# Eight seam norms of a recurrent diffusion backbone, computed with tokens on partitions instead of channels

## The chip, the core and the metric

The kernel runs on one core of a Trainium2 chip. The metric is device time in microseconds (us) of one execution; the profile is that of one profiled execution of the same program, its stretches given in us from the start of its span. Engines are named as in the profile: PE (matmuls), PEld (their weight loads), DVE, ACT, POOL, and the DMA queues SPq and POOLq.

## What is computed

Two groups of tokens, 128 of a context and 512 of a latent grid, pass through two layers of 1024 channels. Each layer is twice the same frame: a norm, a large block (three recurrent mixers, or a gated feed-forward net), and a gated residual. After both layers comes a last norm.

```python
def rmsnorm(x, w):
    y = x * lax.rsqrt(jnp.mean(x * x, axis=-1, keepdims=True) + EPS)
    return y * w

def trunk_layer(x, cvec, lp, init, rows):
    sh1, sc1, g1, sh2, sc2, g2 = jnp.split(silu(cvec) @ lp["w_ada"] + lp["b_ada"], 6)
    h = rmsnorm(x, lp["norm1"]) * (1 + sc1) + sh1
    mix, states = mixer(h, lp, init, rows)
    x = x + g1 * mix
    h = rmsnorm(x, lp["norm2"]) * (1 + sc2) + sh2
    a, b = jnp.split(h @ lp["w_gu"], 2)
    return x + g2 * ((silu(a) * b) @ lp["w_down"]), states
# after two layers: rmsnorm(x, norm_f)
```

The mean is over the 1024 channels of a token. The mixer also uses `a = -exp(s_a_log)`.

## The kernel before

Channels lie on partitions, tokens on columns: `x[k]` (k = 0 to 7) is a 128 x 640 tile of 128 channels by all 640 tokens, and every matmul takes 320 columns, half of the tokens (`HALF`; half 0 holds the context and the first 192 latent tokens, half 1 the rest). Large products are made in three matmuls each, with weights split in a high and a low part (`wh`, `wl`, made by one ACT and one DVE instruction of 128 x 1024) and inputs split likewise.

A **seam** is where one block's output product meets the next norm. There are four: behind the mixers of layer 0 and of layer 1 (the norm then feeds the feed-forward tiles `ga`), behind the feed-forward net of layer 0 (it feeds the first mixer tiles `xT`, `BT` of layer 1), and behind that of layer 1 (the final norm, `final`, whose results are stored). `add_back` makes a seam: it projects eight output tiles `ab`, and behind each, `residual` (DVE) updates `x[f]` and `accumulate_square` adds its square to `ss`: Square on ACT into `sq`, then a DVE add. The last two tiles are projected half by half (`half_major`): first half 0 of both, then half 1 of both.

The norm itself is `rstd_half` (L202), once per half, so eight in all at the seams. A matmul with a constant 128 x 128 tile of 1/1024 (`C_MEAN`) sums `ss` over the partitions and leaves the mean on all 128 partitions at once (`nrm`, 128 x 320); ACT takes Ln of it and Exp of -0.5 times that, into `rstd`. The mixers' inner norm calls it too, on `ssy`.

`first_half` calls it after `2 * n + NSTEP0` steps of `half_major`, so between the matmuls of half 1 of tile 6. A step is three matmuls. What reads `rstd` is a modulator (`modulator`, `block_modulator`): for each k of a half a DVE multiply (`first`, `x<-x,sc,rstd` or `hn<-x,sc,rstd`), an ACT shift that writes the high part (`hb` or `hh`), and a DVE instruction that makes the low part (`second`). In half 0 the multiply is two instructions, of 128 and of 192 tokens, and so are the others; in half 1 it is one of 320.

`second_half` is called inside the next block: three of its tiles are begun together (`together`), half 0 of their tokens first, and after `NSTEP` = 7 steps of the 24 of that half PE does the norm of half 1. In the final seam it follows the last `ab` matmul.

The order of PE's instructions is that of the program's text (`manual_schedule`); at the seams DVE and ACT are ordered by a scheduler when the program is built. `in_order` stamps keep some ACT instructions in the written order, and table loads are asked for ahead of time (`warm_ln`, and behind modulator step `KPRE`). `bank` gives PSUM tiles in turn from a pool of four.

```python
in_order(act.activation(out=r[:, sl], in_=pt[:, :HALF], func=AF.Ln, bias=eps, scale=1.0))
e = act.activation(out=r[:, sl], in_=r[:, sl], func=AF.Exp, scale=-0.5)
```

Of the kernel before, what the change touches and what calls it, by code (L numbers as in the profile page):

```python
# [11 lines left out]
AF = mybir.ActivationFunctionType  # L12
# [4 lines left out]
P = 128  # L17
# [59 lines left out]
NBG = dict(S=3,H=1,M=0)  # L77
LAGB, LAGC, YA, YB = 2,3,2,2
NLEAD = 2
KPRE = 4  # L80
NSTEP0 = 5
ASTART = 38
APRIO = -100
# [25 lines left out]
def backbone(ctx, tc, a):  # L109
# [82 lines left out]
    def accumulate_square(state, x_, hf, sl, first):  # L192
        if first:
            act.activation(out=state[:, sl], in_=x_[:, sl], func=AF.Square)
        else:
            sq = ut("sq")
            last = act.activation(out=sq[:, sl], in_=x_[:, sl], func=AF.Square)
            if ending and hf:
                in_order(last)
            dve.tensor_tensor(out=state[:, sl], in0=state[:, sl], in1=sq[:, sl], op=ALU.add)  # L200

    def rstd_half(r, ssum, hf):  # L202
        sl = halves[hf][1]
        pt = bank("nrm")
        pe.matmul(pt[:, :HALF], cc[:, C_MEAN, :], ssum[:, sl], start=True, stop=True)
        in_order(act.activation(out=r[:, sl], in_=pt[:, :HALF], func=AF.Ln, bias=eps, scale=1.0))
        e = act.activation(out=r[:, sl], in_=r[:, sl], func=AF.Exp, scale=-0.5)
        if ending:
            in_order(e)

    ending = []

    def in_order(ins):
        tc.stamp_issue_order_token(ins.ins, "ln_exp")
# [7 lines left out]
    def warm_ln(src):  # L222
        w = small("warm", 1)
        in_order(act.activation(out=w, in_=src, func=AF.Square))
        in_order(act.preload_act_table(AF.Ln))

    pending = []
    issued = []
# [364 lines left out]
    def modulator(i, x, which, staged=False):  # L593
# [36 lines left out]
        def half(hf, r):  # L630
            sl = halves[hf][1]
            segments = ((0, slice(0, CTX)), (1, slice(CTX, HALF))) if hf == 0 else ((1, sl),)
            ts = {}

            def first(k):
                if k % 2 == 0:
                    ts["t"] = ut("hn")
                ts[k] = ts["t"][:, (k % 2) * HALF : (k % 2 + 1) * HALF]
                if hf == 0:
                    out.append((ut("hh", F32R), ut("hl", F32R)))  # L640
                for j, s2 in segments:
                    s0 = slice(s2.start - sl.start, s2.stop - sl.start)
                    dve.scalar_tensor_tensor(
                        out=ts[k][:, s0], in0=x[k][:, s2], scalar=scv[:, k, j : j + 1], in1=r[:, s2], op0=ALU.mult, op1=ALU.mult
                    )
                    a_ = act.activation(
                        out=out[k][0][:, s2], in_=ts[k][:, s0], func=AF.Identity, bias=mods[i][:, base + k, j : j + 1], scale=1.0
                    )
                if hf == 0 and k == KPRE:
                    in_order(a_)  # L650
                    in_order(act.preload_act_table(AF.Ln))

            def second(k):
                for j, s2 in segments:
                    s0 = slice(s2.start - sl.start, s2.stop - sl.start)
                    dve.scalar_tensor_tensor(
                        out=out[k][1][:, s2], in0=ts[k][:, s0], scalar=mods[i][:, base + k, j : j + 1],
                        in1=out[k][0][:, s2].bitcast(F32), op0=ALU.add, op1=ALU.subtract,
                    )

            first(0)
            for k in range(KT):
                if k + 1 < KT:
                    first(k + 1)
                second(k)
                yield
# [3 lines left out]
    def block_modulator(i, x, pool):  # L670
# [12 lines left out]
        def half(hf, r):  # L683
            sl = halves[hf][1]
            segments = ((0, slice(0, CTX)), (1, slice(CTX, HALF))) if hf == 0 else ((1, sl),)

            def first(k):
                for j, s2 in segments:
                    s0 = slice(s2.start - sl.start, s2.stop - sl.start)
                    dve.scalar_tensor_tensor(  # L690
                        out=x[k][:, s2], in0=x[k][:, s2], scalar=scv[:, k, j : j + 1], in1=r[:, s2], op0=ALU.mult, op1=ALU.mult
                    )
                    a_ = act.activation(out=blocks[k][hf][:, s0], in_=x[k][:, s2], func=AF.Identity, bias=shift(k, j), scale=1.0)
                if hf == 0 and k == KPRE:
                    in_order(a_)
                    in_order(act.preload_act_table(AF.Ln))

            def second(k):
                for j, s2 in segments:
                    s0 = slice(s2.start - sl.start, s2.stop - sl.start)  # L700
                    s1 = slice(s0.start + HALF, s0.stop + HALF)
                    dve.scalar_tensor_tensor(
                        out=blocks[k][hf][:, s1], in0=x[k][:, s2], scalar=shift(k, j),
                        in1=blocks[k][hf][:, s0].bitcast(F32), op0=ALU.add, op1=ALU.subtract,
                    )

            first(0)
            for k in range(KT):
                if k + 1 < KT:
                    first(k + 1)  # L710
                second(k)
                yield
# [35 lines left out]
    def mixers(i, h, ssum, spill, starter, spill_x, first_tickets):  # L748
# [61 lines left out]
        def gates():  # L810
# [17 lines left out]
            dt = gt("gdt", 32)  # L828
            dve.tensor_scalar(out=dt, in0=z[:, :, 8:40], scalar1=0.0, scalar2=None, op0=ALU.max)
            dve.scalar_tensor_tensor(out=dt, in0=q[:, :, 8:40], scalar=2.0, in1=dt, op0=ALU.mult, op1=ALU.add)  # L830
            aexp = small("aexp", 32)
            act.activation(out=aexp, in_=pr[i][:, 48:80], func=AF.Exp)
            dta = gt("gdta", 32)
            dve.scalar_tensor_tensor(
                out=dta, in0=dt, scalar=-1.0, in1=aexp.unsqueeze(1).to_broadcast([P, NCH, 32]), op0=ALU.mult, op1=ALU.mult
# [746 lines left out]

    def add_back(x, tickets, xs, gate, ssum, by_half=False, norm=None, keep=None, home=None, tail=None):
        n = len(xs)

        def want(f):
            for f_ in range(f, min(f + 3, KT)):
# [3 lines left out]
        def done_of(f):  # L1591
            def done(pt, hf, sl):
                residual(x[f], pt, hf, gate, f)
                if ssum is not None:
                    accumulate_square(ssum, x[f], hf, sl, f == 0)
                    if f == KT - 2 and hf == 0:
                        warm_ln(x[f][:, 0:1])
                if keep is not None:
# [14 lines left out]
            return None  # L1613
        fs = range(KT - 2, KT)
        last = half_major([tickets[f] for f in fs], n, xs, "ab", [done_of(f) for f in fs])
        r = ut("rstd")
        lead = norm(0, r)

        def first_half():
            if norm is final:  # L1620
                ending.append(1)
            rstd_half(r, ssum, 0)
            if norm is final:
                return
            for _ in range(NLEAD):
# [1 line left out]

        run(started(last, 2 * n + NSTEP0, first_half))
        if norm is final:
            in_order(act.preload_act_table(AF.Ln))  # L1630
            rstd_half(r, ssum, 1)
            run(lead, final(1, r))
            return None
        run(lead)

        def second_half():
            rstd_half(r, ssum, 1)
            run(norm(1, r))

        return second_half  # L1640
# [85 lines left out]
    def late_constants():  # L1726
# [8 lines left out]
        for i in range(DEPTH):  # L1735
            dve.tensor_tensor(out=hex_[:, i, :], in0=hlb[:, i, :], in1=hmx, op=ALU.subtract)
        act.activation(out=hex_, in_=hex_, func=AF.Exp)
        hsum = cst.tile([P, 8], F32, name="hsum")
        dve.tensor_tensor(out=hsum, in0=hex_[:, 0, :], in1=hex_[:, 1, :], op=ALU.add)
        dve.reciprocal(out=hsum, in_=hsum)  # L1740
# [272 lines left out]
```

## Time and profile before

| | |
|---|---|
| Time, median of 3 runs | 2795.47 us (2792.24 to 2796.05) |
| The profiled execution's own time | 2792.9 us |
| Its span | 2791.1 us |
| PE busy | 2745.5 us (98%) |
| PEld busy | 2697.5 us |
| DVE busy | 1910.1 us (68%) |
| ACT busy | 1234.0 us (44%) |
| Mean granted TensorE clock | 0.997 of 2.4 GHz |

Times outside the span (1.8 us here) belong to the start and the end of the execution. In the timeline, one row merges instructions of the same kind that follow each other: its first number is the start of the first, its second the time to the end of the last. A number in brackets is the time that the engine was idle before, and what ended it. Matmuls overlap, so the time that one costs PE is the distance to the next start, not its duration. An fp32 matmul stands as two in the rows, since PE makes it in two passes, each with a weight load.

### The profile page before, as it was taken

To read this page: it belongs to the slowest core of one execution; us is meant where nothing else is said; L and a number is where in the kernel's file an instruction comes from. 1 tells how busy PE (TensorE), PEld (TensorE's weight loads), DVE (VectorE), ACT (ScalarE), POOL (GpSimd) and SP (SyncE) were. 2 spreads that over 40 slices of the span, in tenths; PEclk is the share of its full clock that TensorE was granted. 3 is DMA by queue.
4 is the path that set the end of the run, shared out by engine and by line. 5 is a ranking of instruction groups with operands and counts; after the bars stand their busy time and mean duration, and the time that the engine had idled before them with its cause. 6 is when DMAs were issued, how large, how long until landed. Compare 5 with 4: busy or idle time off the path is not lost.

```text
span 2791.1 us, 48673 instructions
## 1 busy us (share of the span) xinstructions
PE 2745.5 (98%) x19262; PEld 2697.5 (97%) x19262; DVE 1910.1 (68%) x3822; ACT 1234.0 (44%) x2468; POOL 277.2 (10%) x474
## 2 busy tenths in 40 slices
PE   7999999999999999999999999999999999999998
PEld 6999999999999999999999999999999999999998
DVE  6657668777655586867776665888775556747475
ACT  5545434455542363342455544344455226425243
POOL 0111100000031100000001111000101200000000
PEclk9999999999999999999999999999999999999999
DMA  8444433433474314344534444334344732333433
GB/s 310 133 117 136 117 99 115 132 122 127 140 265 146 106 62 158 125 131 155 176 102 122 126 123 135 115 115 132 122 125 149 248 107 92 100 128 105 131 108 96
DMA packets 119299, 373.42 MB, mean 134 GB/s; under 512 B 16072, under 2 KB 28688, under 8 KB 118944
## 3 DMA queue, kind: packets, MB, share of 16 engines
q1 hardware_dynamic: 92720, 269.56, 30.9%
q0 software_dynamic: 26352, 100.76, 10.6%
q8 instruction: 151, 2.47, 0.4%
q14 instruction: 76, 0.62, 0.1%
HBM read 316.04 MB, written 54.21 MB: 133 GB/s over the span
## 4 chain that ended last, share of the span: by engine, by line
PE 93%; DVE 3%; ACT 2%; DMA 1%; issue 1%; SPq 0%; ACTq 0%; DVEq 0%
PE ga L422 17%; PE ab L494 15%; PE bg L494 12%; PE br L494 8%; PE hfp L494 4%; PE sz L494 4%; PE xT L494 4%; PE hl L1305 3%; PE ga L494 2%; PE hgp L494 2%; PE hqp L494 2%; PE BT L494 2%; PE mkp L494 2%; PE CT L494 2%; PE mop L494 2%; PE mqp L494 1%
## 5 line engine op out<-in xcount | busy, mean ns | idle before, releaser
L411 ACT ACTIVATE wh<-wr 128x1024 fp32r<-128x1024 f32 (+3 forms) x354 | 351.5, 996 | 552.5 <-PE br L494 144.0
L412 DVE TENSOR_TENSOR wl<-wr,wh 128x1024 fp32r<-128x1024 f32 (+3 forms) x354 | 409.2, 1157 | 192.0 <-ACT wh L411 187.5
L422 PE MATMUL ga<-hb,wh 128*128 128x320 f32 x912 | 201.5, 308 | 0.0
L1562 DVE SCALAR_TENSOR_TENSOR x<-ab,hg,x 128x128 f32<-128x128 f32 (+2 forms) x192 | 73.2, 434 | 170.1 <-PE ab L494 170.1
L422 PE MATMUL ga<-hth,wl 128*128 128x320 f32 x608 | 187.8, 309 | 0.0
L422 PE MATMUL ga<-hth,wh 128*128 128x320 f32 x608 | 187.7, 309 | 0.0
L422 PE MATMUL ga<-htl,wh 128*128 128x320 f32 x608 | 187.7, 309 | 0.0
L494 PE MATMUL bg<-hh,wh 128*128 128x320 f32 x768 | 187.2, 325 | 0.0
L494 PE MATMUL bg<-hl,wh 128*128 128x320 f32 x768 | 174.8, 309 | 0.0
L494 PE MATMUL bg<-hh,wl 128*128 128x320 f32 x768 | 174.7, 308 | 0.0
L494 PE MATMUL ab<-uh,wh 128*128 128x320 f32 x704 | 164.7, 310 | 0.0
L494 PE MATMUL ab<-uh,wl 128*128 128x320 f32 x704 | 164.2, 309 | 0.0
L494 PE MATMUL ab<-ul,wh 128*128 128x320 f32 x704 | 164.1, 309 | 0.0
L422 PEld LDWEIGHTS ga<-hb,wh 128*128 128x128 f32 x912 | 152.4, 188 | 0.0
L422 PE MATMUL ga<-hb,wl 128*128 128x320 f32 x456 | 140.6, 308 | 0.0
L494 PEld LDWEIGHTS bg<-hl,wh 128*128 128x128 f32 x768 | 128.6, 188 | 0.0
L494 PEld LDWEIGHTS bg<-hh,wl 128*128 128x128 f32 x768 | 128.5, 188 | 0.0
L494 PEld LDWEIGHTS bg<-hh,wh 128*128 128x128 f32 x768 | 126.2, 189 | 2.1 <-issue 0.8
L494 PEld LDWEIGHTS ab<-ul,wh 128*128 128x128 f32 x704 | 118.8, 188 | 0.2
L494 PEld LDWEIGHTS ab<-uh,wh 128*128 128x128 f32 x704 | 118.7, 188 | 0.2
L494 PEld LDWEIGHTS ab<-uh,wl 128*128 128x128 f32 x704 | 118.5, 188 | 0.0
L1153 ACT ACTIVATE E<-E,gsb 128x128 f32<-128x128 f32 x320 | 99.8, 392 | 38.1 <-POOL E L943 38.0
(497 smaller groups left out, 7538.2 us busy)
## 6 DMA issues: line engine op xcount, KB each, us to landing
wr<-w_in SPq DMA_DIRECT2D x152, 512.0 KB, 3.5
wr<-w_gu SPq DMA_DIRECT2D x88, 512.0 KB, 3.6
wa<-w_ada SPq DMA_DIRECT2D x84, 512.0 KB, 3.4
E<-rows_s SPq DMA_DIRECT2D x80, 256.0 KB, 5.8
x<-xd POOLq DMA_DIRECT2D x64, 320.0 KB, 3.7
wr<-w_down SPq DMA_DIRECT2D x32, 512.0 KB, 3.9
sp<-bgt POOLq DMA_DIRECT2D x48, 320.0 KB, 3.6
bgr<-sp POOLq DMA_DIRECT2D x48, 320.0 KB, 4.7
```

Of the source, the lines that this page charges most:

```text
L411: act.activation(out=hi[:, :n], in_=raw[:, :n], func=AF.Copy)
L412: dve.tensor_tensor(out=lo[:, :n], in0=raw[:, :n], in1=hi[:, :n].bitcast(F32), op=ALU.subtract)
L422: pe.matmul(bank_[:, :HALF], a_[:, sl], b_, start=first and j == m == 0, stop=j == n - 1 and m == 2, skip_group_check=True,)
L494: pe.matmul(out[hf][:, :HALF], wt_[:, sl], b_, start=m == k == 0, stop=m == 2 and k == n - 1)
L1153: act.activation(out=e[:, j * P : (j + 1) * P], in_=e[:, j * P : (j + 1) * P], func=AF.Exp, bias=gv["sb"][:, d, c, 4 * g + j : 4 * g + j + 1],
L1305: pe.matmul(pt[:, (c - c0) * P : (c - c0 + 1) * P], kk[:, sl], halves_of(QK[:, 0, sl], 3 * T, L, P // (2 * L)), start=True, stop=True,)
L1562: dve.scalar_tensor_tensor(out=x_[:, lo:hi], in0=pt[:, lo - hf * HALF : hi - hf * HALF], scalar=gate[:, 2 * f + j : 2 * f + j + 1], in1=x_ ...
```

## The change

The eight norms at the seams are made by a new function `rstd_seam`. The mean is taken with tokens on partitions: for each of three groups of 128 tokens (0 to 127, 128 to 255, and 192 to 319 of the half) the 128 x 128 block of squares is the weight and one column of `C_MEAN` is what moves, so the result is one column of 128 tokens. It does so for `ss` and for the square of the last tile, which is no longer added into `ss` on DVE. ACT takes Sqrt of the three columns (128 x 3), DVE the reciprocal, and three fp32 matmuls with the identity, with each column repeated 128 times as the weight, spread the result over all partitions again, into a PSUM tile `nrb` of 320 columns. The modulators read it there. The table that is asked for ahead is that of Sqrt; the requests behind step `KPRE` are gone. The Exp of `s_a_log` is made once for both layers in `late_constants`. `rstd_half` stays for the mixers' inner norm.

```diff
+    def rstd_seam(r, parts, hf):
+        t0 = hf * HALF
+        starts = (0, P, HALF - P)
+        pt = bank("nrm")
+        for c, s0 in enumerate(starts):
+            for n, part in enumerate(parts):
+                pe.matmul(
+                    pt[:, c : c + 1], part[:, t0 + s0 : t0 + s0 + P], cc[:, C_MEAN, 0:1], start=n == 0, stop=n == len(parts) - 1
+                )
+        s = small("rt", 3)
+        in_order(act.activation(out=s, in_=pt[:, 0:3], func=AF.Sqrt, bias=eps, scale=1.0))
+        dve.reciprocal(out=s, in_=s)
+        bc = r.of[hf] = bank("nrb")
+        for c, s0 in enumerate(starts):
+            c0 = max(s0, c * P)
+            n = min(P, HALF - c0)
+            pe.matmul(
+                bc[:, c0 : c0 + n], s[:, c : c + 1].to_broadcast([P, P]), ident[:, c0 - s0 : c0 - s0 + n], start=True, stop=True
+            )
...
-        in_order(act.preload_act_table(AF.Ln))
+        in_order(act.preload_act_table(AF.Sqrt))
...
-                if hf == 0 and k == KPRE:
-                    in_order(a_)
-                    in_order(act.preload_act_table(AF.Ln))
...
-            aexp = small("aexp", 32)
-            act.activation(out=aexp, in_=pr[i][:, 48:80], func=AF.Exp)
+            aexp = pr[i][:, 48:80]
...
-                    accumulate_square(ssum, x[f], hf, sl, f == 0)
+                    if f == KT - 1 and norm is not None:
+                        if hf == 0:
+                            last_sq.append(ut("sq"))
+                        act.activation(out=last_sq[0][:, sl], in_=x[f][:, sl], func=AF.Square)
+                    else:
+                        accumulate_square(ssum, x[f], hf, sl, f == 0)
...
-            rstd_half(r, ssum, 0)
+            rstd_seam(r, (ssum, last_sq[0]), 0)
...
-            rstd_half(r, ssum, 1)
+            rstd_seam(r, (ssum, last_sq[0]), 1)
```

On PE, at the norm of half 1 behind the mixers of layer 0 (`ga` are the feed-forward tiles, `hb` their input of half 0, `mr` and `ab` lie before). Before:

```order
L494 MATMUL ga_10662<-hb_10055,wh_10519 128x320 x2
L494 MATMUL ga_10662<-hb_10055,wl_10520 128x320
L205 MATMUL nrm_10689<-ss_10048,cc 128x320
L494 MATMUL ga_10667<-hb_10055,wh_10523 128x320 x2
L494 MATMUL ga_10667<-hb_10055,wl_10524 128x320
```

With the change:

```order
L516 MATMUL ga_10667<-hb_10055,wl_10519 128x320
L213 MATMUL nrm_10694<-cc,ss_10048 128x1
L213 MATMUL nrm_10694<-cc,sq_10540 128x1
L213 MATMUL nrm_10694<-cc,ss_10048 128x1
L213 MATMUL nrm_10694<-cc,sq_10540 128x1
L213 MATMUL nrm_10694<-cc,ss_10048 128x1
L213 MATMUL nrm_10694<-cc,sq_10540 128x1
L223 MATMUL nrb_10704<-cc,rt_10701 128x128 x2
L223 MATMUL nrb_10704<-cc,rt_10701 128x64
```

Where one matmul stood, nine stand now, and the last three read `rt`, which ACT and DVE write from the first six. The `ga` matmuls of half 0 that are left follow behind them.

On DVE, at the same place: the end of the modulator's half 0 and the start of its half 1 (`x` is the residual stream, scaled in place; `hb` the split input of the feed-forward tiles). Before:

```order
L702 SCALAR_TENSOR_TENSOR hb_10065<-x_9684,mod_86,hb_10065 128x128
L702 SCALAR_TENSOR_TENSOR hb_10065<-x_9684,mod_86,hb_10065 128x192
L690 SCALAR_TENSOR_TENSOR x_9455<-x_9455,sc_10049,rstd_10467 128x320
L690 SCALAR_TENSOR_TENSOR x_9487<-x_9487,sc_10049,rstd_10467 128x320
L690 SCALAR_TENSOR_TENSOR x_9522<-x_9522,sc_10049,rstd_10467 128x320
```

With the change:

```order
L718 SCALAR_TENSOR_TENSOR hb_10063<-x_9652,mod_86,hb_10063 128x128
L718 SCALAR_TENSOR_TENSOR hb_10063<-x_9652,mod_86,hb_10063 128x192
L718 SCALAR_TENSOR_TENSOR hb_10065<-x_9684,mod_86,hb_10065 128x128
L718 SCALAR_TENSOR_TENSOR hb_10065<-x_9684,mod_86,hb_10065 128x192
L218 RECIPROCAL rt_10701<-rt_10701 128x3
L709 SCALAR_TENSOR_TENSOR x_9455<-x_9455,sc_10049,nrb_10704 128x320
L709 SCALAR_TENSOR_TENSOR x_9487<-x_9487,sc_10049,nrb_10704 128x320
```

The reciprocal of half 1 stands behind every DVE instruction of half 0 of the modulator. It stands so at all three seams that feed another block.

## Rows read from the trace of the kernel before

**Rows 1.** The page, part 1: busy time of each engine.

```profile
PE 2745.5 (98%) x19262; PEld 2697.5 (97%) x19262; DVE 1910.1 (68%) x3822; ACT 1234.0 (44%) x2468; POOL 277.2 (10%) x474
```

**Rows 2.** Waits of PE over the whole span: us in total, times, longest.

```profile
PE ga L494 <- DVE hb L702: 3.3, 8, 0.8
...
PE xT L494 <- ACT hh L646: 1.8, 1, 1.8
```

**Rows 3.** Timeline of PE, norm of half 0 behind the mixers of layer 0.

```profile
966.35 0.70 PE L205 MATMUL nrm<-ss,cc 128*128 128x320 f32 x2
966.64 0.70 PE L494 MATMUL ab<-mr,wh 128*128 128x320 f32 x2
967.18 0.31 PE L494 MATMUL ab<-mr,wl 128*128 128x320 f32 x1
```

**Rows 4.** Timeline of PE around small fp32 matmuls of 20 and of 128 columns.

```profile
180.06 0.29 PE L905 MATMUL mend<-gmc,cc 128*128 128x20 f32 x2
180.20 0.38 PE L906 MATMUL mend<-gmc,cc 128*128 128x20 f32 x2
180.42 0.54 PE L494 MATMUL bg<-hh,wh 128*128 128x320 f32 x2
...
109.24 0.83 PE L1098 MATMUL cb<-CT,sA 128*128 128x128 f32 x6
```

**Rows 5.** Tiles `mend` and `den`: durations in ns, min/median/max.

```profile
L907 ACT ACTIVATE gme<-mend x2: 204/204/205, 180.6 to 1552.3; 128x40 f32<-128x40 f32 x2
...
L1455 DVE RECIPROCAL den<-den x40: 157/166/167, 643.0 to 2134.4; 128x2 f32<-128x2 f32 x40
```

**Rows 6.** Timeline of DVE behind the mixers of layer 0: first and last of half 0, first of half 1.

```profile
969.43 1.27 DVE L690 SCALAR_TENSOR_TENSOR x<-x,sc,rstd 128x128 f32<-128x128 f32 x4 [0.47 <-ACT rstd L207]
...
981.35 1.26 DVE L702 SCALAR_TENSOR_TENSOR hb<-x,mod,hb 128x128 fp32r<-128x128 f32 x4
983.90 1.48 DVE L690 SCALAR_TENSOR_TENSOR x<-x,sc,rstd 128x320 f32<-128x320 f32 x3 [1.28 <-ACT rstd L207]
```

**Rows 7.** Timeline of PE, same seam: norm of half 1, second `ga` matmul of half 1.

```profile
976.56 0.70 PE L205 MATMUL nrm<-ss,cc 128*128 128x320 f32 x2
...
985.89 0.41 PE L494 MATMUL ga<-hb,wh 128*128 128x320 f32 x1 [0.23 <-DVE hb L702]
```

**Rows 8.** Timelines of DVE and PE, the seam between the layers.

```profile
1408.88 0.55 DVE L1562 SCALAR_TENSOR_TENSOR x<-ab,hg,x 128x320 f32<-128x320 f32 x1 [0.30 <-PE ab L494]
1409.34 1.26 DVE L643 SCALAR_TENSOR_TENSOR hn<-x,sc,rstd 128x128 f32<-128x128 f32 x4
...
1416.07 1.21 DVE L412 TENSOR_TENSOR wl<-wr,wh 128x1024 fp32r<-128x1024 f32 x1
...
1420.04 1.40 DVE L656 SCALAR_TENSOR_TENSOR hl<-hn,mod,hh 128x128 fp32r<-128x128 f32 x4 [0.38 <-ACT hh L646]
...
1404.93 0.81 PE L205 MATMUL nrm<-ss,cc 128*128 128x320 f32 x2
...
1414.83 0.70 PE L205 MATMUL nrm<-ss,cc 128*128 128x320 f32 x2
...
1423.63 0.31 PE L494 MATMUL xT<-hh,wh 128*128 128x320 f32 x1
```

**Rows 9.** PE at a mixer's `val`: its wait; then 76-79 us (busy times, granted clock).

```profile
74.53 0.38 PE L1042 MATMUL val<-wh,hh 128*128 128x304 f32 x1 [3.43 <-DVE cu L1002]
...
76.00:79.00 3.00, 3.00 (x13) 3.00 (x13) 0.40 (x1) 0.21 (x2) 0.00 (x0) 0.50 0.00 0
```

**Rows 10.** The end: last `ab` matmul, Ln and table load, the last multiplies.

```profile
2778.04 0.31 PE L494 MATMUL ab<-uh,wl 128*128 128x320 f32 x1
...
2781.28 0.53 ACT L206 ACTIVATE rstd<-nrm,eps 128x320 f32<-128x320 f32 x1 [0.42 <-PE nrm L205]
2781.83 1.28 ACT L207 ACT_TABLE_LOAD   x1
...
2783.63 3.79 DVE L1570 SCALAR_TENSOR_TENSOR x<-x,normf,rstd 128x320 f32<-128x320 f32 x8 [0.93 <-ACT rstd L207]
```

More of the change, by code (lines that the diff above doesn't have):

```diff
@@ L79 @@
 NLEAD = 2
-KPRE = 4
 NSTEP0 = 5
@@ L196, in accumulate_square, with __init__, __getitem__ @@
             sq = ut("sq")
-            last = act.activation(out=sq[:, sl], in_=x_[:, sl], func=AF.Square)
-            if ending and hf:
-                in_order(last)
+            act.activation(out=sq[:, sl], in_=x_[:, sl], func=AF.Square)
             dve.tensor_tensor(out=state[:, sl], in0=state[:, sl], in1=sq[:, sl], op=ALU.add)
+    class Columns:
+        def __init__(self):
+            self.of = {}
+        def __getitem__(self, key):
+            hf = int(key[1].start >= HALF)
+            return self.of[hf][:, key[1].start - hf * HALF : key[1].stop - hf * HALF]
+    def rstd_seam(r, parts, hf):
[17 more added lines that the diff above has]
+            )
     def rstd_half(r, ssum, hf):
@@ L206, in rstd_half @@
         in_order(act.activation(out=r[:, sl], in_=pt[:, :HALF], func=AF.Ln, bias=eps, scale=1.0))
[L207 to L211, printed above, removed]
+        act.activation(out=r[:, sl], in_=r[:, sl], func=AF.Exp, scale=-0.5)
     def in_order(ins):
@@ L645, in first @@
                     )
-                    a_ = act.activation(
+                    act.activation(
                         out=out[k][0][:, s2], in_=ts[k][:, s0], func=AF.Identity, bias=mods[i][:, base + k, j : j + 1], scale=1.0
                     )
-                if hf == 0 and k == KPRE:
-                    in_order(a_)
-                    in_order(act.preload_act_table(AF.Ln))
             def second(k):
@@ L692, in first @@
                     )
[L693 to L696, printed above, removed]
+                    act.activation(out=blocks[k][hf][:, s0], in_=x[k][:, s2], func=AF.Identity, bias=shift(k, j), scale=1.0)
             def second(k):
@@ L1584, in add_back @@
         n = len(xs)
+        last_sq = []
         def want(f):
@@ L1615, in add_back @@
         last = half_major([tickets[f] for f in fs], n, xs, "ab", [done_of(f) for f in fs])
-        r = ut("rstd")
+        r = Columns()
         lead = norm(0, r)
         def first_half():
-            if norm is final:
-                ending.append(1)
-            rstd_half(r, ssum, 0)
+            rstd_seam(r, (ssum, last_sq[0]), 0)
             if norm is final:
@@ L1629, in add_back @@
         if norm is final:
-            in_order(act.preload_act_table(AF.Ln))
-            rstd_half(r, ssum, 1)
+            rstd_seam(r, (ssum, last_sq[0]), 1)
             run(lead, final(1, r))
@@ L1636, in second_half @@
         def second_half():
-            rstd_half(r, ssum, 1)
+            rstd_seam(r, (ssum, last_sq[0]), 1)
             run(norm(1, r))
@@ L1737, in late_constants @@
         act.activation(out=hex_, in_=hex_, func=AF.Exp)
+        for i in range(DEPTH):
+            act.activation(out=pr[i][:, 48:80], in_=pr[i][:, 48:80], func=AF.Exp)
         hsum = cst.tile([P, 8], F32, name="hsum")
```

## The prediction, made before the changed kernel ran

> **What bounds the kernel now.** The page's first part comes first: PE is busy 98% of the span, DVE 68%, ACT 44% [rows 1]. So the time is PE's instructions plus the little that PE waits, and an edit is worth what it puts on PE or makes PE wait. The list of PE's waits comes next: at the seams PE loses 3.3 us in eight waits for `hb` and 1.8 us in one for `hh` [rows 2]; that is about all that a quicker norm could give back there. Then the timelines of PE and DVE at the seams show what each norm costs. The norm of half 0 takes PE's place of an `ab` step, and DVE's modulator starts behind it [rows 3, 6]. The norm of half 1 is made early: `nrm` stands at 976.56, while DVE is still in half 0 of the modulator until 981.35 + 1.26 = 982.61 [rows 6, 7]. PE does not care, for it has 17 steps of half 0 left and reads nothing of the norm itself.
>
> **The price of a small pass.** The old `nrm`: from 966.35 to the third start behind it at 967.18 are 0.83 us, less two `ab` matmuls of 0.15 each, so 0.54 us [rows 3]. The change puts 12 passes of one column and 6 of 64 to 128 columns there. Nearest rows: four passes of 20 columns move the next start by 180.42 - 180.06 = 0.36 us, 0.09 each; six of 128 columns last 0.83 us to the last end, and as two passes last 0.29, of which one step is 0.09, the last needs 0.20 to end, which leaves 0.63 / 5 = 0.12 or 0.13 a step [rows 4]. I take 0.11 for all and keep 0.09 and 0.13 for the range; a far upper end is `nrm`'s own 0.27 a pass [rows 3].
> The Trainium skill's "TensorE: Matmul & The Clock Gate", section "Back-to-back issue gap", gives about 81 ns as the sustained spacing of a weight load and matmul of 128 columns. By it the 18 passes would be an estimated 0.5 us shorter per norm; the rows of fp32 passes are longer, and they decide.
>
> **Half 0, mixer seams.** New on PE: 12 passes, 11 x 0.11 + 0.20 until the last ends = 1.41; Sqrt on three columns, as a small ACT instruction, 0.20, with 0.05 before it; reciprocal 0.17 [rows 5]; 0.2 for hand-over and weight load (an estimate, no row has it alone); 6 passes 0.66. Together 2.7 us in place of 0.54: PE goes on **2.2 us** later, because `nrb` stands in its stream ahead of the rest of half 1 of `ab` and must wait for ACT and DVE. DVE's first multiply comes at 966.35 + 2.9 = about 969.3, as before (969.43) [rows 3, 6]: Ln, table load and Exp are gone, but that gain is eaten by the passes. So no wait of PE for `hb` ends earlier.
>
> **Half 1, mixer seams (two).** Here PE, DVE and the written order meet. The excerpt of DVE's order shows the reciprocal of half 1 behind every instruction of half 0 of the modulator; `nrb` waits for it, and 17 of the 24 steps of half 0, which wait for nothing in it, stand behind `nrb`. DVE's block of half 0 is 982.61 - 969.43 = 13.2 us [rows 6]; one 128 x 320 residual more and one add into `ss` less leave it at that. So: 969.3 + 13.2 = 982.5, reciprocal until 982.7, hand-over and passes 0.86, PE goes on at 983.6. A step of three matmuls is 0.44 us: 2745.5 us of PE over 19262 matmuls are 0.143 each [rows 1], at this seam 0.15 [rows 3]. The 17 steps take 7.5 us, so half 1 starts at 991.1. Before, it began one matmul ahead of 985.89, at 985.74 [rows 7]. That is **+5.3 us** a seam, the 2.2 of half 0 and some PE waits for `hb` inside the 17 steps included. (Without waits the old start would be 976.56 + 0.54 + 7.5 = 984.6; the missing 1.1 us are those waits.)
>
> **The seam between the layers.** Half 0: `nrm` at 1404.93 delays PE by 2.2 us as well, but PE waited 1.8 us for `hh` there [rows 2, 8], so that hides nearly all of it. DVE starts its multiplies at 1404.93 + 2.9 = 1407.9, before at 1409.34. Its block was 1409.34 to 1421.44, 12.1 us, with 0.38 of waiting; in the new order one `wl` (1.2) and two residuals (0.46 each) have come into it and an add (0.4) has left, so 13.4 us [rows 8]. Reciprocal done 1421.5, PE goes on at 1422.4, half 1 starts at 1429.9 against 1423.63: **+6.2 us**.
>
> **TensorE's clock.** In the three stalls of half 1 PE has nothing but the twelve tiny passes to do for 5 us or so. The trace shows what came after a stop of 3.43 us: in the stretch 76 to 79 the granted clock was 0.50, the 1.2 GHz level, with 13 matmuls in 3.0 us, 0.23 each where 0.15 is the pace [rows 3, 9], so a loss of 13 x 0.08 = 1.1 us, a little more with the edges of the stretch: 1.3. I count 3 x 1.3 = **3.9 us**. Ends: nothing, if the clock stays; twice that, if it stays low longer, and as much again if the shorter stops of half 0 lower it too.
>
> **The final seam.** PE's last `ab` comes 2.2 us later than 2778.04. Behind it: table load, Exp and hand-over, 2783.63 - 2781.83 = 1.80, are gone; Ln 0.53 becomes Sqrt 0.20; the add into `ss`, about 0.47, is gone; ten passes in place of `nrm` add 0.56; reciprocal, hand-over and `nrb` add 1.03. The multiplies start 2.2 - 1.80 - 0.33 - 0.47 + 0.56 + 1.03 = **+1.2 us** late, and they end the span [rows 10].
> The Trainium skill's "ScalarE: Activation LUTs", section "What ACT_TABLE_LOAD costs", puts a change of table at about 2.66 us with a drain. By it the tail would gain an estimated 1.4 us more; in the row the load is 1.28 us and what follows starts at once.
>
> **Counted as nothing.** ACT's removed loads elsewhere, Ln and Exp: ACT is idle over half the time, and no PE wait at a seam but the one for `hh` is for it. The Exp of `s_a_log` moves to the constants; one ACT instruction of 32 columns. Multiplies with an operand in PSUM: the residual, which reads `ab` from there, takes 0.55 for 128 x 320 and the multiply from SBUF 1.48 for three, 0.49 [rows 6, 8]; up to 0.06 x 8, and PE is not behind these.
>
> **The sum.** 2 x 5.3 + 6.2 + 3.9 + 1.2 = 21.9 us. Against the profiled execution, 2792.9, that is 2814.8; it lies 2.6 below the median of the three runs (2795.47), which would give 2817.4. I take the middle, **2816**. About 0.2% (5.6 us) is what a measurement of this kernel can tell from no change.
>
> **Rivals.**
> - *The stalls cost more.* The clock stays low twice as long behind half 1 (+3.9) and falls in the stops of half 0 too (+3.9), or the broadcast passes cost 0.27 (6 x 0.16 x 7 norms = +6.7): 2823 to 2831. For it: PE's stop is longer than the one of rows 9. Against: that one had ended its loss in about 3.4 us, and the passes of rows 4 are short. Chance 0.12.
> - *No stall in half 1.* Only passes and hand-over count: 2.2 for two norms of half 0, 2.2 for three of half 1, less the PE waits they fill (1.1 twice, 0.8 at the layers), plus 1.2: 9.2, so about 2803. It needs the reciprocal to come early on DVE; the order shows it last. Chance 0.12.
> - *Faster: the shorter ACT path empties PE's waits.* If DVE's block of half 0 were over before PE comes to `nrb`, at about 978 behind the mixers, and the passes cost no more than the old `nrm`, the 3.3 + 1.8 us of waits [rows 2] would go, and the tail would gain 1.0: 2788. It decides at a block of under 978 - 969.3 = 8.7 us, which takes 13.2 now. Chance 0.04.
> - *Not done as written*: table loads between Sqrt, Square and Identity would put 1.28 us each on ACT; the order of the changed kernel has none there. No chance of its own.
>
> **How the numbers follow.** My forecast has 0.72. Its own bounds: without clock loss (-3.9), with passes at 0.09 (18 x 0.02 in four stretches, -1.5) and on the profiled execution's footing (-1.2), 2809; with passes at 0.13 (+1.5), half as much clock loss again (+1.9) and on the median's footing (+1.4), 2821. To leave no more than 2 in 10 out, the range goes down to the middle of the case without stall and up nearly to the end of the dear stalls: 2803 to 2830. It leaves out the faster rival (0.04), the lower half of the case without stall (0.06) and the very end of the dear one. Faster by over 0.2% is that rival, 0.04. Within 0.2% (2789.9 to 2801.1) lies that lower half, 0.06, where the passes are cheap and the clock stays. Slower: 0.90.
>
> **What would show it.** Right: new waits of PE at `nrb` on DVE's reciprocal, about 0.5 us in half 0 and 4 to 6 us in three norms of half 1; the reciprocal of half 1 directly behind the last `hb` of half 0; granted clock 0.5 for some 3 us behind; starts of `nrb` passes about 0.11 apart; the last multiplies 1 us late against the last `ab`'s own shift. Wrong: reciprocal of half 1 before the end of DVE's half 0; no PE wait over 2 us there; clock near 1 throughout; or DVE's multiplies of half 0 starting over 1 us sooner at the mixers, with `hb` waits gone.

## The result, and the profile after

| | before | with the change |
|---|---|---|
| Time, median of 6 runs each on the same chip | 2794.56 us | 2816.57 us (2814.49 to 2819.34) |
| Ratio | | 1.0076, 95% interval 1.0066 to 1.0086 |
| Span of the profiled execution | 2791.1 us | 2815.0 us |

The change costs 22 us, 0.8%. The forecast was 2816.0 us, its range 2803 to 2830. One execution of the run e_rec below took 4522.7 us, a slow one at a granted clock of 0.556, and its median is that of the other eight.

First the page of the changed kernel, engines and busy time, as in [rows 1]:

```profile
PE 2761.9 (98%) x19390; PEld 2719.0 (97%) x19390; DVE 1906.2 (68%) x3822; ACT 1215.4 (43%) x2449; POOL 280.7 (10%) x474
```

PE is still busy 98% of the span, ACT has 19 us less work, DVE 4 us less. By these shares nothing went wrong. The list of PE's waits (total, times, longest) says more; it answers to [rows 2]:

```profile
PE nrb L223 <- DVE rt L218: 12.4, 7, 4.8
...
PE nrb L223 <- DVE gmp L929: 5.4, 1, 5.4
...
PE xT L516 <- ACT hh L642: 1.4, 1, 1.4
```

The first two entries are new: PE waits 17.8 us at `nrb`, for the reciprocals `rt`. (The 5.4 us carry the name `gmp` because two tiny memsets follow the reciprocal directly on DVE; PE starts 0.14 us behind that reciprocal.) The waits of `ga` for `hb`, 3.3 us in [rows 2], are gone from the list. The third line is not the wait between the layers of [rows 2]: it lies at 25 us, ahead of the first mixers. Between the layers PE no longer waits for `hh`; the first `xT` starts 0.15 us behind the start of the last `ab`:

```profile
1417.34 0.31 PE L516 MATMUL ab<-uh,wl 128*128 128x320 f32 x1
1417.49 0.31 PE L516 MATMUL xT<-hh,wh 128*128 128x320 f32 x1
```

The timeline of PE behind the mixers of layer 0, norm of half 0, then norm of half 1 (answers to [rows 3, 7]):

```profile
965.81 0.28 PE L213 MATMUL nrm<-cc,ss 128*128 128x1 f32 x2
965.95 0.36 PE L213 MATMUL nrm<-cc,sq 128*128 128x1 f32 x2
966.18 0.36 PE L213 MATMUL nrm<-cc,ss 128*128 128x1 f32 x2
...
967.77 0.88 PE L223 MATMUL nrb<-cc,rt 128*128 128x128 f32 x6 [0.56 <-DVE rt L218]
968.46 0.54 PE L516 MATMUL ab<-mr,wh 128*128 128x320 f32 x2
...
978.00 0.28 PE L213 MATMUL nrm<-cc,ss 128*128 128x1 f32 x2
...
979.03 0.36 PE L213 MATMUL nrm<-cc,sq 128*128 128x1 f32 x2
984.16 1.52 PE L223 MATMUL nrb<-cc,rt 128*128 128x128 f32 x6 [4.77 <-DVE rt L218]
985.44 0.88 PE L516 MATMUL ga<-hb,wh 128*128 128x320 f32 x2
```

In half 0 the norm takes 968.46 - 965.81 = 2.65 us of PE. In half 1 the twelve mean passes are over at about 979.4, and PE then stands until 984.16. DVE shows why (answers to [rows 6]):

```profile
968.69 1.25 DVE L709 SCALAR_TENSOR_TENSOR x<-x,sc,nrb 128x128 f32<-128x128 f32 x4 [0.97 <-PE nrb L223]
...
971.72 1.23 DVE L434 TENSOR_TENSOR wl<-wr,wh 128x1024 fp32r<-128x1024 f32 x1 [0.60 <-ACT wh L433]
...
975.12 0.55 DVE L1577 SCALAR_TENSOR_TENSOR x<-ab,hg,x 128x320 f32<-128x320 f32 x1 [1.12 <-PE ab L516]
...
982.67 1.26 DVE L718 SCALAR_TENSOR_TENSOR hb<-x,mod,hb 128x128 fp32r<-128x128 f32 x4
983.85 0.16 DVE L218 RECIPROCAL rt<-rt 128x3 f32<-128x3 f32 x1
```

ACT's Sqrt for it was over at 979.69:

```profile
979.43 0.26 ACT L217 ACTIVATE rt<-nrm,eps 128x3 f32<-128x3 f32 x1 [0.85 <-PE nrm L213]
```

So the reciprocal waits only for its turn, behind the last `hb` of half 0. The windows of the same seam (us, then busy time and count of PE, PEld, DVE, ACT, POOL; then granted clock, DMA share, GB/s), with [rows 9] as the one to compare:

```profile
968.50:972.20 3.70, 3.70 (x17) 3.70 (x17) 2.91 (x9) 2.64 (x6) 0.00 (x0) 0.56 0.00 0
978.00:984.10 6.10, 1.39 (x14) 1.30 (x12) 6.01 (x19) 4.71 (x14) 0.00 (x0) 0.88 0.26 86
984.10:990.00 5.90, 5.84 (x25) 5.87 (x26) 4.27 (x10) 3.70 (x8) 0.00 (x0) 0.55 0.00 0
```

The clock is down twice: behind the stall of half 1, and, for a shorter time, behind the norm of half 0, where PE waited just 0.56 us but ran eighteen tiny passes.

To compare kernels, one length per seam serves: from the first mean matmul to a matmul that comes after the seam in every version (behind the mixers the first of the twin products, L422 before and L444 with the change; between the layers the first of tile `CT`). For layer 0 those are, before and with the change:

```profile
1019.12 0.46 PE L422 MATMUL ga<-hb,wh 128*128 128x320 f32 x2
```

```profile
1026.38 0.46 PE L444 MATMUL ga<-hb,wh 128*128 128x320 f32 x2
```

So 1019.12 - 966.35 = 52.8 us before [rows 3], 1026.38 - 965.81 = 60.6 us now. All seams, from the profiled executions (the experiments' rows are read the same way; the last column is made from unrounded lengths). One execution can lie some us off its median: that of e_rec took 2797.2 us where the median is 2801.6, that of e_slack1 2788.2 where it is 2792.7.

| us | mixers 0 | between layers | mixers 1 | three seams against before |
|---|---|---|---|---|
| before | 52.8 | 29.3 | 52.9 | |
| the change | 60.6 | 37.8 | 60.7 | +24.2 |
| e_rec | 54.7 | 31.2 | 54.7 | +5.6 |
| e_fill | 56.6 | 36.8 | 58.2 | +16.7 |
| e_old0 | 57.4 | 36.0 | 58.0 | +16.5 |
| e_old1 | 59.1 | 39.5 | 60.8 | +24.4 |
| e_old1b | 54.1 | 30.8 | 55.7 | +5.7 |
| e_late_both | 55.5 | 31.5 | 54.0 | +6.1 |
| e_slack | 52.5 | 31.2 | 52.5 | +1.3 |
| e_slack1 | 51.6 | 30.1 | 51.5 | -1.7 |

The end of the changed kernel, as in [rows 10]: last `ab` matmul, then the last multiplies.

```profile
2803.24 0.31 PE L516 MATMUL ab<-uh,wl 128*128 128x320 f32 x1
...
2804.75 0.38 PE L213 MATMUL nrm<-cc,sq 128*128 128x1 f32 x2 [1.08 <-ACT sq L1614]
...
2806.59 0.88 PE L223 MATMUL nrb<-cc,rt 128*128 128x128 f32 x6 [0.56 <-DVE rt L218]
```

```profile
2807.51 3.75 DVE L1585 SCALAR_TENSOR_TENSOR x<-x,normf,nrb 128x320 f32<-128x320 f32 x8 [0.54 <-PE nrb L223]
```

From the last `ab` to the multiplies it is 4.27 us now, 5.59 before: 1.3 us won there, against 2.2 lost in the final seam's half 0.

### The profile page after: what moved, and what is told of

It is laid out like the page before. It is cut to its first block, busy times and chain, and to the rows that moved or that the text cites. A ratio compares the mean times of both kernels' runs of the same rounds, so it can differ in the third digit from the quotient of the medians.

```text
span 2815.0 us, 48933 instructions
## 1 busy us (share of the span) xinstructions
PE 2761.9 (98%) x19390; PEld 2719.0 (97%) x19390; DVE 1906.2 (68%) x3822; ACT 1215.4 (43%) x2449; POOL 280.7 (10%) x474
## 4 chain that ended last, share of the span: by engine, by line
PE 94%; DVE 3%; ACT 1%; DMA 1%; issue 1%; SPq 0%; DVEq 0%; ACTq 0%
PE ga L444 17%; PE ab L516 15%; PE bg L516 12%; PE br L516 8%; PE hfp L516 4%; PE sz L516 4%; PE xT L516 4%; PE ga L516 3%; PE hl L1320 2%; PE hgp L516 2%; PE hqp L516 2%; PE BT L516 2%; PE mkp L516 2%; PE CT L516 2%; PE mop L516 1%; PE mqp L516 1%
## 5 line engine op out<-in xcount | busy, mean ns | idle before, releaser
L444 PE MATMUL ga<-hb,wh 128*128 128x320 f32 x912 | 201.2, 308 | 0.0
L444 PE MATMUL ga<-hth,wl 128*128 128x320 f32 x608 | 187.9, 309 | 0.0
L444 PE MATMUL ga<-hth,wh 128*128 128x320 f32 x608 | 187.5, 308 | 0.0
L444 PE MATMUL ga<-htl,wh 128*128 128x320 f32 x608 | 187.4, 308 | 0.0
L444 PEld LDWEIGHTS ga<-hb,wh 128*128 128x128 f32 x912 | 152.4, 188 | 0.0
L444 PE MATMUL ga<-hb,wl 128*128 128x320 f32 x456 | 140.5, 308 | 0.0
```

Source lines behind the costliest of these rows:

```text
L444: pe.matmul(bank_[:, :HALF], a_[:, sl], b_, start=first and j == m == 0, stop=j == n - 1 and m == 2, skip_group_check=True,)
```

## The experiments

Diffs are against the changed kernel unless said otherwise. Each median has that of the kernel before, from the same chip and runs, beside it.

**e_rec: the reciprocal early on DVE.**

```diff
-        dve.reciprocal(out=s, in_=s)
+        with tc.high_priority(offset=300):
+            dve.reciprocal(out=s, in_=s)
```

> Only the place of DVE's reciprocal of half 1 changes: it moves 14 instructions up, into the middle of half 0 of the modulator. Theory Q (the stall is the queue: nrb waits because the reciprocal stands behind DVE's half 0): PE's wait at nrb of half 1 falls from 4.8 us to under 1 us, the clock does not drop behind it, and the seams give back about 3.3 + 6.0 + 3.3 us: about 2804 us. Theory B (nrb of half 1 also waits for the bank of nrb of half 0, which is free only after the last multiply of half 0): that multiply now ends about 983.4, so the wait stays at 4 us or more and only 1 to 2 us come back: about 2815 us. Theory P (every norm costs the same, some 2.7 us, for its passes and hand-overs, wherever DVE stands): no change, 2816.6 us.

Measured: 2801.6 us (before 2793.8), ratio 1.0028, interval 1.0018 to 1.0038. One line: 7.9 us above the kernel before in place of 22.0, so 14 us back. DVE and PE at the same place as above:

```profile
976.70 0.34 DVE L710 SCALAR_TENSOR_TENSOR x<-x,sc,nrb 128x128 f32<-128x128 f32 x1
977.81 0.18 DVE L219 RECIPROCAL rt<-rt 128x3 f32<-128x3 f32 x1 [0.77 <-ACT rt L217]
...
981.11 0.67 DVE L710 SCALAR_TENSOR_TENSOR x<-x,sc,nrb 128x128 f32<-128x128 f32 x2
981.69 1.27 DVE L719 SCALAR_TENSOR_TENSOR hb<-x,mod,hb 128x128 fp32r<-128x128 f32 x4
```

```profile
978.13 0.85 PE L224 MATMUL nrb<-cc,rt 128*128 128x128 f32 x6 [0.66 <-DVE rt L219]
```

Theory Q holds: the wait is 0.66 us where it was 4.77. Theory B falls: `nrb` starts at 978.13, while half 0 is still multiplied until about 981.8; no bank held it. One part of Q's forecast missed: the clock did fall behind this norm, to 0.72 over the stretch 978 to 984 (its row is in the last section).

**e_rec_one: the same with mean and broadcast in one bank.**

```diff
-                    pt[:, c : c + 1], part...
+                    pt[:, HALF + c : HALF + c + 1], part...
...
-        bc = r.of[hf] = bank("nrb")
+        bc = r.of[hf] = pt
```

> As the run before, DVE's order the same, and the mean and the broadcast share one PSUM bank, so nrb of half 1 no longer takes the bank that nrb of half 0 leaves. Q and B both say: PE's wait at nrb of half 1 about 0.6 us, granted clock near 1 behind it, about 2804 us. If the run before is already at 2804, the bank was nothing. P: 2816.6 us.

Measured: 2801.9 us, ratio 1.0030 (1.0019 to 1.0041): the same as e_rec. The bank is nothing for the time.

**e_fill: work in the stall that nobody reads.** `feeds` is true for half 1 at the three feeding seams.

```diff
+        if feeds and hf:
+            for _ in range(8):
+                pe.matmul(pt[:, 8 : 8 + HALF], cc[:, C_MEAN, :], parts[0][:, halves[hf][1]], start=True, stop=True)
         bc = r.of[hf] = bank("nrb")
```

> Three times (half 1, the three seams that feed a block) eight fp32 matmuls of 320 columns, 0.54 us each, stand between the mean and nrb; their result is read by no one. They lie inside the stall, so PE goes on when it did, but it was busy in between. Theory C (the clock is part of the loss: 5.4 us at half rate behind each of the three stalls, 2.7 us each): granted clock near 1 behind nrb of half 1, 8 us less: about 2808.5 us. If the clock costs only what the prediction took (1.3 us each): 2812.7 us. If the time behind the stall is set by something else: 2816.6 us or a little more.

Measured: 2810.4 us (before 2793.8), ratio 1.0059 (1.0046 to 1.0071). PE does 24 matmuls more, and the kernel is 16.6 us above the kernel before in place of 22.0. The stall is filled, and the clock behind it stays up:

```profile
977.97 4.58 PE L221 MATMUL nrm<-ss,cc 128*128 128x320 f32 x16 [0.35 <-ACT rt L217]
982.40 0.85 PE L226 MATMUL nrb<-cc,rt 128*128 128x128 f32 x6
...
982.40:988.40 6.00, 6.00 (x43) 6.00 (x43) 5.09 (x11) 4.52 (x9) 0.00 (x0) 1.00 0.02 7
```

So the clock is part of the loss, 5.4 us or on average 1.8 for each of the three stalls: between the 1.3 of the prediction and the 2.7 of theory C. It is no clean 8 us. Between the layers the clock fell while the fill itself ran:

```profile
1420.00:1422.00 2.00, 2.00 (x4) 1.25 (x5) 1.94 (x7) 1.42 (x5) 0.00 (x0) 0.50 0.00 0
```

There the eight matmuls took 6.1 us in place of 4.4 and kept `nrb` back 1.2 us beyond the reciprocal; that seam keeps 36.8 us.

**e_old1: half 1 in the old way, with a slip of mine.** In the old kernel the last square is added into `ss` on DVE; here that add was written at the place of the norm. (The request for Ln's table behind step `KPRE` is back as well, here and in e_old1b.)

```diff
         def second_half():
-            rstd_seam(r, (ssum, last_sq[0]), 1)
+            o = ut("rstd")
+            r.of[1] = o[:, HALF:T]
+            dve.tensor_tensor(out=ssum[:, HALF:T], in0=ssum[:, HALF:T], in1=last_sq[0][:, HALF:T], op=ALU.add)
+            rstd_half(o, ssum, 1)
```

> Half 1 of the three feeding seams is made in the old way (one mean matmul, Ln, Exp, no nrb), half 0 and the final norm in the new one. Q: the stalls and their clock loss go; left are the first halves (about 2 us at each mixer seam, nearly nothing between the layers) and 1 us at the end: about 2800 us. P (all eight norms cost alike): three eighths of 22 us come back, 2808 us.

Measured: 2822.2 us (before 2793.8), ratio 1.0102 (1.0087 to 1.0117): worse than the change. PE's waits of this kernel:

```profile
PE nrm L230 <- DVE ss L1663: 13.4, 2, 6.7
...
PE nrm L230 <- DVE gmp L935: 6.3, 1, 6.3
```

DVE behind the mixers of layer 0, the last `hb` of half 0 and the new add:

```profile
982.44 0.42 DVE L724 SCALAR_TENSOR_TENSOR hb<-x,mod,hb 128x192 fp32r<-128x192 f32 x1 [0.29 <-ACT hb L715]
982.78 0.48 DVE L1663 TENSOR_TENSOR ss<-ss,sq 128x320 f32<-128x320 f32 x1
```

The expectation missed because the edit made the very thing it was to remove: the scheduler put the new add behind all of DVE's half 0, where the reciprocal had stood. It is the sharpest evidence for Q all the same. There is no `nrb`, no pass of one column and no reciprocal in half 1 here, and PE waits 6.7 us: only the place in DVE's queue is common to both.

**e_old1b: the same with the add where it was.** The last square goes through `accumulate_square` again in half 1, at the residual.

```diff
-                    if f == KT - 1 and norm is not None:
+                    if f == KT - 1 and norm is not None and made_new(hf):
...
+            o = ut("rstd")
+            r.of[1] = o[:, HALF:T]
+            rstd_half(o, ssum, 1)
```

> Half 1 in the old way at the three feeding seams, as in e_old1, but its last square is added into ss where the kernel before adds it (behind the residual, in the middle of DVE's half 0) and not in a new instruction behind all of half 0. Half 0 and the final norm stay new. Q (the stall is whatever PE waits for behind DVE's half 0): the 6.7 us waits of e_old1 at nrm go, left are the first halves (about 1.5 us at a mixer seam with its clock loss, 0.5 between the layers) and 1 us at the end: about 2798 us. P (all eight new norms cost alike, 2.7 us): 2808 us. If the old norm itself costs more beside the new half 0, for table loads: near e_old1, 2820 us.

Measured: 2802.1 us (before 2794.0), ratio 1.0028 (1.0019 to 1.0037). 20 us between two kernels that differ in where one 0.48 us add stands. P's 2808 lies 4 us above the interval (2799 to 2804), Q's 2798 one below it. The seams' lengths give +5.7 and the final one about 1, that is about 2801.

**e_old0: half 0 in the old way, half 1 new.**

```diff
-            rstd_seam(r, (ssum, last_sq[0]), 0)
+            if made_new(0):
+                rstd_seam(r, (ssum, last_sq[0]), 0)
+            else:
+                o = ut("rstd")
+                r.of[0] = o[:, :HALF]
+                rstd_half(o, ssum, 0)
```

> The other way round: half 0 in the old way at the three feeding seams, half 1 and the final norm in the new one, the reciprocal of half 1 left behind DVE's half 0. Q: three stalls of 4 to 5 us with their clock loss stay, only what the first halves add goes: about 2812 us. P: 2808 us. If the first halves and their clock loss are the larger part: below 2803 us.

Measured: 2814.8 us (before 2794.0), ratio 1.0071 (1.0059 to 1.0084). Nearly all of the loss is still there with half 0 restored: three halves 1 carry it, as Q says. In the profiled execution the three seams hold 16.5 us of the 20.9 and the end some 3, where the clock fell behind the new half 0 of the final norm; the rest is not placed. The wait at the same place is as long as in the change:

```profile
983.78 1.54 PE L223 MATMUL nrb<-cc,rt 128*128 128x128 f32 x6 [4.75 <-DVE rt L218]
```

**e_late_both: `nrb` later in PE's order, DVE left alone.** `rstd_seam` ends before the broadcast and returns it as a function `spread`; half 1 calls it 13 steps later, half 0 three.

```diff
+LATE = 13
+LATE0 = 3
...
-        run(started(last, 2 * n + NSTEP0, first_half))
+        k0 = 2 * n + NSTEP0
+        run(started(started(last, k0, first_means), k0 + LATE0, first_half))
...
+        return lambda g: started(started(g, NSTEP, means), NSTEP + LATE, second_half)
```

> The change with the same instructions, DVE's reciprocals where they are, but the nrb matmuls later in PE's order: 13 steps of ga or xT behind the mean in half 1, 3 steps of ab in half 0. PE has work while ACT and DVE make the columns. Q: no wait of PE over 0.5 us at nrb at the feeding seams, granted clock 1.0 there; PE pays passes alone, 18 x 0.11 - 0.54 = 1.4 us for seven norms, less the old waits for hb and hh that these fill (4 us) and 2.3 us of the tail: about 2798 us. P: passes and hand-overs cost the same anywhere, 2816 us. If a later nrb starves half 1 (its first hb comes too late): waits for hb of 1 us and more, 2802 us.

Measured: 2801.3 us (before 2794.0), ratio 1.0029 (1.0019 to 1.0039). The other end of the same wait moves, and 14.7 us come back. The waits at `nrb` are gone but for the one in the final seam, and half 1 isn't starved. The clock did not stay at 1.0 everywhere, though Q had it so: behind the mean of half 1 at the mixers of layer 0 it was 0.59 (last section). What takes some of it back stands elsewhere: PE waits 1.5 us at each mixer seam for an `hb` of half 0, whose multiplies now start later, and behind a `wl` that the scheduler puts ahead of them.

```profile
PE ga L521 <- DVE hb L723: 3.0, 2, 1.5
...
PE nrb L226 <- DVE rt L220: 0.6, 1, 0.6
```

**e_final1: the new norm only at the very end** (half 1 of the final seam; all other norms old, with Sqrt's table asked for between the Exp of half 0 and the last Square).

```diff
         if norm is final:
+            in_order(act.preload_act_table(AF.Sqrt))
             rstd_seam(r, (ssum, last_sq[0]), 1)
```

> The new norm at one place only: half 1 of the final seam, where nothing is left for PE behind it. All else as before. From the last ab matmul to the first multiply of the last half 5.6 us before, 4.3 us with the change: 1.3 us less than before, 2792.5 us where before is at 2793.8. If the gain at the end is taken back by the table load that must now come between Exp and Sqrt: no change.

Measured: 2796.5 us (before 2794.0), ratio 1.0008 (1.0000 to 1.0017). A miss. ACT at the end:

```profile
2784.42 0.46 ACT L196 ACTIVATE sq<-x 128x320 f32<-128x320 f32 x1
2784.89 1.28 ACT L1665 ACT_TABLE_LOAD   x1
2786.19 0.47 ACT L1625 ACTIVATE sq<-x 128x320 f32<-128x320 f32 x1
```

The table load now stands before the last Square, and in this mix the last multiplies begin 2790.24 - 2784.94 = 5.3 us behind the last `ab` matmul: 0.3 won of the 1.3. That it came out above the kernel before isn't explained by this; in its profiled execution, the slowest of its eleven, the mixers of layer 1 took some 4 us longer and the three seams, though their norms are the old ones, 1.7 us. I leave that open.

**e_slack: both remedies.** The reciprocal as in e_rec, `nrb` as in e_late_both, but half 1 only two steps later.

```diff
+LATE = 2
+LATE0 = 3
...
+        with tc.high_priority(offset=300):
+            dve.reciprocal(out=s, in_=s)
```

> All of the change's instructions, with both remedies: the reciprocal early on DVE (as in e_rec) and nrb later in PE's order, 2 steps behind the mean in half 1 and 3 steps in half 0, so that PE has work while ACT and DVE make the columns. Q: no wait of PE at nrb at the feeding seams, granted clock 1.0 there, half 1 not starved (the waits for hb of 1.5 us that e_late_both showed are gone): e_rec and e_late_both each left 7 to 8 us over the kernel before, of which the passes are 7 x 1.4 = 10 us less the old waits filled (about 5) and less the tail (2); about 2797 us. If half of what is left were hand-over waits that stay: 2801 us.

Measured: 2795.9 us (before 2795.0), ratio 1.0004 (0.9996 to 1.0013): no difference from the kernel before. The same instructions as in the change, in another order, are worth 21 us. Windows of this kernel behind the mean of half 0 and behind `nrb` of half 1, where the change had 0.56 and 0.55:

```profile
968.50:974.00 5.50, 5.50 (x41) 5.50 (x41) 4.15 (x11) 3.18 (x7) 0.54 (x1) 1.00 0.20 56
979.80:985.80 6.00, 6.00 (x44) 6.00 (x43) 6.00 (x17) 4.30 (x13) 0.00 (x0) 1.00 0.29 87
```

**e_slack1: as e_slack, with half the mean passes** in seven norms.

```diff
-                    if f == KT - 1 and norm is not None:
-                        if hf == 0:
-                            last_sq.append(ut("sq"))
+                    if f == KT - 1 and norm is final and hf:
+                        last_sq.append(ut("sq"))
...
-            rstd_seam(r, (ssum, last_sq[0]), 0)
+            rstd_seam(r, (ssum,), 0)
```

> As e_slack, but for seven of the eight norms the last square is added into ss on DVE as before, so a norm takes 6 mean passes in place of 12 (half 1 of the final seam keeps 12). If a pass is 0.11 us of PE: 7 x 6 x 0.11 = 4.6 us under e_slack. If the passes hide in other work: the same as e_slack; if the add makes PE wait: above it.

Measured: 2792.7 us (before 2795.0), ratio 0.9993 (0.9984 to 1.0002). 3.2 us under e_slack for 42 passes, 0.08 us a pass; the expectation was 4.6. It may be a little quicker than the kernel before; the interval does not exclude that it is the same. PE still waits for `hb` at each mixer seam:

```profile
PE ga L522 <- DVE hb L724: 1.5, 2, 0.7
```

**e_slack2: e_slack1 with `LATE0 = 2`.**

> e_slack1 with nrb of half 0 two steps behind the mean in place of three. There PE had no wait at nrb and a wait of 0.7 us for hb at each mixer seam, 1.4 for hh between the layers, all set by when DVE's half 0 starts; a step earlier is 0.44 us for each of the three: 1.3 us under e_slack1's 2792.7, so about 2791.4 us, which would lie below the kernel before (2795.0). If DVE or ACT is not done two steps behind the mean, PE waits at nrb and nothing is gained: 2792.7 us or more.

Measured: 2793.1 us (before 2794.4), ratio 0.9995 (0.9986 to 1.0004): nothing gained. PE does not wait at `nrb` in these seams, yet its wait for `hb` at the mixer seams is still 0.8 us, so the earlier broadcast did not shorten it.

**e_aexp: the kernel before with the moved Exp alone.**

```diff
-            aexp = small("aexp", 32)
-            act.activation(out=aexp, in_=pr[i][:, 48:80], func=AF.Exp)
+            aexp = pr[i][:, 48:80]
...
+        for i in range(DEPTH):
+            act.activation(out=pr[i][:, 48:80], in_=pr[i][:, 48:80], func=AF.Exp)
```

> The kernel before with one edit of the change alone: Exp of s_a_log once for both layers among the constants. The prediction counted it as nothing: within 1 us of before. If it shifts the order of ACT and DVE in the mixers for the worse: 2 to 3 us more, which would also be the 2.5 us that e_final1 lies above before.

Measured: 2794.3 us (before 2795.0), ratio 0.9997 (0.9988 to 1.0006): nothing, as counted.

## Why the prediction was right

The mechanism is the one forecast, and it is shown from both ends: the reciprocal's place in DVE's queue (e_rec, and e_old1 by accident) and PE's place of `nrb` (e_late_both) each bring the stall or take it away, while passes and banks stay as they are.

- **Half 0.** Forecast 2.7 us in place of 0.54, measured 2.65. Starts of the mean matmuls' rows lie 0.225 apart for two passes, 0.11 each, the price taken between the bounds of [rows 4]. Sqrt took 0.26, not 0.20. The 0.2 for hand-over, for which the prediction had no row, was 0.08: 0.03 us ahead of the reciprocal and 0.05 behind it. DVE's first multiply came 2.88 us behind the first pass, forecast 2.9.
- **Half 1 behind the mixers.** Forecast: PE goes on 983.6 - 966.35 = 17.25 us behind the first mean matmul. Measured 985.44 - 965.81 = 19.6. Two sizes were off, for one reason. DVE's block took 15.2 us (968.69 to 983.93), not 13.2: it waited 1.12 for an `ab` tile and 0.60 for a `wh`. And the six passes of `nrb` took 1.28 us, not 0.66. The clock had fallen, behind half 0 (which delayed that `ab` tile) and during the stall. In e_rec, with the same order there and the clock at 1.00, DVE waits 0.17 for that tile and 0.01 for that `wh`. The old start of half 1 was read a little wrong: its first matmul began at 985.25, and only 0.4 of the 1.1 us of old waits lie inside the 17 steps, the rest at the first two matmuls of half 1. The +5.3 counts from the second one, so it stands.
- **The clock was the term most under-sized.** The prediction had 1.3 us a stall, counted from PE's restart. In 985.44 to 989.51 fifteen matmuls go 0.27 apart where 0.147 is the pace, 1.8 us lost, and `nrb` at half rate loses 0.6 more: 2.4. The case "the shorter stops of half 0 lower it too", kept as a bound only, happened at both mixer seams of this execution. e_fill gives 1.8 us a stall over the medians.
- **What was not counted gave some back.** The old wait of 1.2 us of `ga` for `sa`, once per mixer seam, has vanished from PE's waits: PE now comes later to it than ACT. I had not counted it.
- **Seams.** With the clock the forecast was 6.6, 7.5 and 6.6; measured 7.8, 8.6 and 7.9. At the seam between the layers the delay of half 0 was hidden behind the wait for `hh`, as forecast (first `xT` 5.82 us behind the first mean matmul, 5.74 before).
- **The final seam.** Forecast +1.2: the multiplies start 2807.51 - 2797.57 = 9.94 us behind the first mean matmul of half 0, before 2783.63 - 2774.53 = 9.10 (2797.57 and 2774.53 are those matmuls' starts), so +0.8.
- **The sum.** 21.9 forecast; +23.9 between the two spans, +22.0 between the medians. The number itself, 0.6 us off the median, is nearer than its terms are, and that is partly luck: by the profiled executions the three seams cost 24.2 us and not 20.7, and the medians lie 2 us closer together than those executions.
- **Table loads.** Trace and Trainium skill differ: "ScalarE: Activation LUTs", section "What ACT_TABLE_LOAD costs", gives about 2.66 us with a drain for a change of table; in the rows of e_final1 the Square starts 0.02 us behind the end of the 1.28 us load, and the load 0.01 us behind the Square before it.
- **Rivals.** "No stall in half 1" was priced at 2803 and named its condition, an early reciprocal: e_rec met that condition and ran 2801.6. The "faster" rival did not come even in e_slack1: the waits for `hb` behind the mixers fall from 3.3 us to 1.5 and those seams are 1.2 us shorter than before, but between the layers PE waits 1.4 us for `hh` and 1.1 for `hl`, and that seam is 0.9 us longer.

## What to carry to other kernels

When a step is replaced by a chain over several engines, look where each link stands in its engine's queue and what stands behind the instruction that waits for it: the place of a 0.17 us reciprocal was worth 14 of the 22 us here, because it stood behind 13 us and more of DVE work, and PE's next 7.5 us stood behind its result. Put the urgent small instruction forward and give the waiting engine other work between the two halves of the chain. In an experiment that restores old code, restore its place in every queue too.

## What was not expected of the hardware

In the change the granted clock fell behind the norm of half 0 at both mixer seams (0.56 at the first), where PE waited only 0.56 us. In the kernel before it stayed at full rate around PE's longer wait for `hh` between the layers, 1.8 us [rows 2]; the window around that wait:

```profile
1400.00:1430.00 30.00, 27.48 (x175) 25.64 (x174) 25.15 (x69) 22.13 (x43) 3.74 (x7) 1.00 0.26 82
```

Beside the short wait PE ran twelve passes of one column and six of 64 to 128. It isn't a rule that these lower the clock. Between the layers of the changed kernel the same eighteen passes with the same wait of 0.56 us left it at 1.00; in e_old1, at the same place, it fell. The change, then e_old1, behind the norm of half 0 between the layers:

```profile
1414.50:1418.50 4.00, 3.89 (x27) 3.63 (x26) 3.72 (x10) 3.25 (x6) 0.72 (x2) 1.00 0.07 14
```

```profile
1413.30:1417.30 4.00, 4.00 (x18) 4.00 (x18) 3.76 (x10) 2.33 (x5) 0.00 (x0) 0.58 0.10 15
```

In e_rec the norm of half 0 behind the mixers of layer 0 left it at 1.00, and that of half 1, with a wait of 0.66 us, did not:

```profile
968.00:974.00 6.00, 6.00 (x44) 6.00 (x43) 5.49 (x15) 4.63 (x10) 0.54 (x1) 1.00 0.13 39
978.00:984.00 6.00, 5.87 (x31) 5.90 (x32) 6.00 (x17) 4.20 (x13) 0.00 (x0) 0.72 0.28 87
```

Even within one execution the same instructions gave both levels. In e_late_both PE waits 1.5 us for `hb` in half 0 at each mixer seam, runs a few matmuls and the twelve passes, and goes straight on with matmuls of 320 columns; behind that the clock is down at the mixers of layer 0 and not at those of layer 1:

```profile
979.50:983.50 4.00, 4.00 (x19) 4.00 (x19) 3.49 (x13) 3.79 (x13) 0.00 (x0) 0.59 0.01 4
```

```profile
2354.10:2358.10 4.00, 4.00 (x29) 4.00 (x29) 3.50 (x13) 3.92 (x13) 0.00 (x0) 1.00 0.00 0
```

What decides between the two stays open, so the clock's share of a seam can differ from one execution to the next.

In e_slack, where the same passes run with matmuls of 320 columns in place of the wait, the clock stayed at 1.00 at all three seams that feed a block. In e_fill such matmuls held it there through the stalls behind the mixers, though not between the layers. On the whole PE working for nothing was quicker than PE waiting, 2810.4 us against 2816.6.
